# A build-time list scheduler that may place SBUF arithmetic on either of two engines

## The chip, the cores and the metric

The kernel runs on one core of a Trainium2 chip. The metric is the device time of one execution in microseconds. Five engines work side by side, each from its own queue of instructions in a fixed order: TensorE (PE in the profile; PEld are its weight loads), VectorE (DVE), ScalarE (ACT), GpSimd (POOL) and SyncE (SP), which issues all the DMA transfers of this kernel. An instruction waits for semaphores that other engines raise; everything behind it in its queue waits with it.

## The reference

One inference step of a decoder layer, in float32, for a prompt of 2048 tokens and for 8 decode tokens that share the weights. `D_MODEL` is 1024, the FFN width 2816. Cut to what matters:

```python
def decoder_layer(x, ...):
    y = parallel_mixer(rms_norm(x, norm_mix), ...)     # one input projection, then
                                                       #   group A: GLU, depthwise conv of width 31, layer norm, silu
                                                       #   group B: short conv, gated DeltaNet in chunks, 4 heads
                                                       #   concatenated, one output projection
    x = x + y
    x = x + memory_attend(rms_norm(x, norm_mem_q), mem_k, mem_v, w_mq, w_mo)   # 4 heads, 256 memory tokens
    x = x + swiglu(rms_norm(x, norm_ffn), w_gate, w_up, w_down)
    return x, ...

def swiglu(h, w_gate, w_up, w_down):
    return (jax.nn.silu(h @ w_gate) * (h @ w_up)) @ w_down

y_prompt = rms_norm(xp, norm_f)
y_sample = rms_norm(xs, norm_f)
```

## The kernel before

Activations lie transposed, channels on the 128 partitions and tokens along the free axis. The prompt is cut into four blocks of 512 tokens (`NB`, `TB`). Each large product is made of three matmuls in a reduced-precision float32 format: an operand X is split into a high part, which ScalarE writes as a rounded copy, and a low part X - high, which is a subtraction of 128x512 elements from SBUF to SBUF. So each weight tile goes through three steps: a DMA into a `raw` tile, a copy on ScalarE into the first half of a `w` tile, and the subtraction `w<-raw,w` into the second half. Activations are split in the same way (`hT`, `catS`, `op`, `ff`, `fo`), from PSUM or from SBUF.

The FFN uses a seven-product scheme (Strassen's, in Winograd's form) on halves of the tokens and of the channels: products Q1, Q2, P5, P6, Q3, Q7 and P4 per column step `f` (22 steps per block) go to the PSUM tiles `fx`, `fy`, `fz`, and VectorE adds them up into `ffu` and `ffs`. The sums of weights that the scheme needs are `raw<-raw,raw` and `raw<-raw` additions. Those of gate and up are made once and kept in DRAM as `sums`; those of the down projection are made anew in blocks 1 to 3, four operations of 128x128 in a row (`sums_down`). Beside this stand the convolution (`cacc`, 30 taps of 128x512 on VectorE for each of 16 tiles), the DeltaNet chunks with their small triangular inverses (`bit`, `biq`, `Tm`), the norms (sums of squares `sqj`; a power function that only GpSimd runs, for `rs`, `rs1`, `tbr`, `s12`) and the softmax of the memory attention.

No instruction is issued when its line runs. `hybrid_step` drives a rough model of the clock (`Clock`, `Engine`, `Sched`) that decides what is emitted in which order, and each call lands on a `Tape` as an operation with its engine. The engine is set by the code: `V` for VectorE, `G` for GpSimd, or for weight splits and sums a choice between them by the rough clock (`WS.engine`, `WS.split`, `split_down`, `sums_down`). At the end `Tape.issue` calls `Tape.order`, which simulates the five engines, and all instructions go out in the order that it returns; every profile row therefore bears that line, L479.

`order` is a list scheduler. `graph` finds the dependences; `keys` gives each operation a number by which it is needed (for TensorE its place on the tape; for others the smallest number among what depends on it or wants its buffer, at most `LATER` = 300 behind its own). Each engine has a heap `future` of operations by the time at which they will be ready, and a heap `avail` of ready ones by key. The engine whose clock is lowest takes the ready operation with the smallest key whose tiles are to be had; otherwise the operation is put off (`push`) or parked until a buffer of that kind comes free (`wake`). Times come from `Tape.cost`, which returns nanoseconds, whether the operation uses the SBUF port that VectorE and GpSimd share, and a ScalarE table. Operations that use the port follow one another in the plan (`port_at`). Before, every GpSimd operation other than `memset` and `affine_select` counts as a user, and on VectorE those with two tensor inputs in SBUF (`big > 1`). If VectorE's next operation would wait over 150 ns for the port, one that doesn't use it is taken in its place.

What the order fixes: the sequence on each engine, SP's DMA issues among them. What the plan supposes of times has no force on the chip; there only the semaphores decide.

Names in the profile: `w` weight tiles, `raw` their sources, `tbd`/`tbr` and `dnb` the small broadcast of the decode tokens' norm, `nrs` a scaled copy of a norm, `x` the residual, `dn`, `dx`, `dy`, `dz` products of the down projection, `rg` those of the output and attention projections, `sc` scores, `pss` and `prs` sums of squares and their spread on TensorE.

## Time and profile before

| | |
|---|---|
| median of 3 runs | 2961.06 us (2959.1 to 2961.39) |
| the profiled execution's own time | 2956.49 us |
| its span in the profile | 2954.8 us |
| PE, PEld busy | 2901.7 us, 2606.9 us |
| DVE, ACT, POOL busy | 2135.4 us, 1460.3 us, 1832.3 us |
| share of the DMA queue of 16 engines' span | 60.0% |
| mean granted TensorE clock | 0.994 |

A row of the groups of instructions reads: line, engine, operation, written tile <- read tiles, shapes, count | busy time, mean ns of one | idle time of the engine just before them, and what ended it. A row of the waits reads: who <- for whom: us in total, times, the longest. A row of the order of time reads: start, length, engine, operation, count. The span is what the instructions cover; the execution's own time is 1.7 us longer.

### The profile page before, as it was taken

How to read it: one execution, taken by the hardware profiler on the slowest of the kernel's cores; microseconds unless marked ns; L12 is line 12 of the kernel's file. 1: busy time of each engine (PE TensorE's matmuls, PEld its weight loads, DVE VectorE, ACT ScalarE, POOL GpSimd, SP SyncE). 2: the span in 40 equal slices, each digit the busy share in tenths (PEclk: the TensorE clock that was granted, in tenths of full speed). 3: DMA queues.
4: the chain of work that ended last, by engine and by line, in shares of the span. 5: the costliest groups of instructions: out<-in, count | busy, mean ns of one | idle time of the engine just before them, and what ended most of it. 6: DMA issues, size and time to landing. Idle time of an engine off the chain costs nothing.

```text
span 2954.8 us, 56193 instructions
## 1 busy us (share of the span) xinstructions
PE 2901.7 (98%) x19620; PEld 2606.9 (88%) x19620; DVE 2135.4 (72%) x4265; ACT 1460.3 (49%) x3038; POOL 1832.3 (62%) x1949
## 2 busy tenths in 40 slices
PE   9999999999999999999999999999999999999998
PEld 7999878878887888998887888998988999999998
DVE  8757888979758837957577965666866576776667
ACT  7544556456774445455454443444444444444444
POOL 4554454786656455568666127787513888758887
PEclk9999999999999999999999999999999999999999
DMA  6533435777773325766576777777527666666664
GB/s 216 159 95 111 127 107 161 248 250 247 232 237 117 118 86 191 233 193 213 187 248 235 250 242 224 240 232 235 181 91 221 209 202 189 211 227 195 211 210 127
DMA packets 363036, 569.43 MB, mean 193 GB/s; under 512 B 55840, under 2 KB 158560, under 8 KB 362736
## 3 DMA queue, kind: packets, MB, share of 16 engines
q1 hardware_dynamic: 362752, 565.84, 60.0%
q8 instruction: 155, 2.54, 0.3%
q14 instruction: 129, 1.06, 0.1%
HBM read 457.77 MB, written 108.51 MB: 192 GB/s over the span
## 4 chain that ended last, share of the span: by engine, by line
PE 62%; DMA 2%; DVE 1%; POOL 1%; issue 1%; ACT 1%; SPq 0%; POOLq 0%; DVEq 0%; ACTq 0%
PE fy L479 12%; PE rg L479 11%; PE fz L479 8%; PE fx L479 8%; PE dn L479 6%; PE sc L479 5%; PE dx L479 5%; PE dz L479 3%; PE dy L479 1%; DMA w<-sums 1%; PE pu L479 1%; PE pch L479 1%; POOL w L479 0%; PE ppt L479 0%; DMA raw<-in_w_down_dram 0%
## 5 line engine op out<-in xcount | busy, mean ns | idle before, releaser
L479 POOL TENSOR_TENSOR w<-raw,w 128x512 fp32r<-128x512 f32 (+1 forms) x783 | 1040.4, 1339 | 543.7 <-ACT w L479 518.5
L479 ACT ACTIVATE w<-raw 128x512 fp32r<-128x512 f32 (+1 forms) x1066 | 649.5, 619 | 908.4 <-PE fz L479 95.2
L479 PE MATMUL fy<-op,w 128*128 128x256 f32 (+1 forms) x3168 | 435.0, 283 | 6.7 <-DMA w<-sums 3.0
L479 PEld LDWEIGHTS fy<-op,w 128*128 128x128 f32 x3168 | 400.0, 189 | 14.5 <-DVE ffu L479 3.8
L479 PE MATMUL hd<-hT,w 128*128 128x512 f32 (+2 forms) x1920 | 395.9, 356 | 0.6 <-ACT w L479 0.3
L479 DVE SCALAR_TENSOR_TENSOR cacc<-cu,cw,cacc 128x512 f32<-128x512 f32 x480 | 359.2, 748 | 11.6 <-ACT cacc L479 4.9
L479 PEld LDWEIGHTS hd<-hT,w 128*128 128x128 f32 x1920 | 302.3, 188 | 44.1 <-ACT w L479 0.9
L479 DVE TENSOR_TENSOR w<-raw,w 128x512 fp32r<-128x512 f32 (+1 forms) x283 | 251.1, 891 | 90.8 <-ACT w L479 86.8
L479 PE MATMUL fx<-op,w 128*128 128x256 f32 (+1 forms) x2112 | 300.3, 285 | 3.2 <-ACT ffs L479 2.3
L479 PE MATMUL fz<-op,w 128*128 128x256 f32 (+1 forms) x2112 | 292.0, 284 | 1.6 <-DMA w<-sums 1.5
L479 POOL TENSOR_TENSOR sqj<-sqj,sqj 128x512 f32<-128x512 f32 (+1 forms) x98 | 135.0, 1377 | 252.4 <-ACT sqj L479 250.1
L479 PEld LDWEIGHTS fx<-op,w 128*128 128x128 f32 x2112 | 271.5, 190 | 13.7 <-ACT ffs L479 4.3
L479 PEld LDWEIGHTS fz<-op,w 128*128 128x128 f32 x2112 | 268.6, 190 | 8.0 <-issue 4.8
L479 POOL TENSOR_TENSOR raw<-raw 128x128 f32<-128x128 f32 x336 | 194.5, 590 | 21.2 <-DMA raw<-in_w_down_dram 19.9
L479 PE MATMUL dx<-fo,w 128*128 128x256 f32 (+1 forms) x1344 | 197.0, 284 | 0.1
L479 PE MATMUL dn<-ff,w 128*128 128x512 f32 (+2 forms) x960 | 192.5, 352 | 2.8 <-POOL w L479 1.5
L479 PE MATMUL rg<-pT,w 128*128 128x512 f32 x768 | 190.5, 399 | 0.9 <-ACT pr L479 0.7
L479 PE MATMUL sc<-w,hT 128*128 128x512 f32 x768 | 188.6, 401 | 0.0
L479 PE MATMUL rg<-catS,w 128*128 128x512 f32 (+2 forms) x960 | 186.5, 351 | 0.0
L479 POOL TENSOR_TENSOR raw<-raw,raw 128x128 f32<-128x128 f32 (+1 forms) x183 | 161.5, 884 | 28.2 <-PE dr L479 7.1
L479 PEld LDWEIGHTS dx<-fo,w 128*128 128x128 f32 x1344 | 173.8, 188 | 4.0 <-DVE x L479 1.2
L479 PEld LDWEIGHTS rg<-catS,w 128*128 128x128 f32 x960 | 154.4, 188 | 24.6
(401 smaller groups left out, 5060.1 us busy)
## 6 DMA issues: line engine op xcount, KB each, us to landing
w<-sums SPq DMA_DIRECT2D x222, 512.0 KB, 4.3
raw<-in_w_gate_dram SPq DMA_DIRECT2D x192, 256.0 KB, 3.3
sums<-w SPq DMA_DIRECT2D x66, 512.0 KB, 3.8
raw<-in_w_up_dram SPq DMA_DIRECT2D x118, 256.0 KB, 3.6
raw<-in_w_down_dram SPq DMA_DIRECT2D x224, 128.0 KB, 2.7
raw<-in_w_in_dram SPq DMA_DIRECT2D x96, 256.0 KB, 3.2
raw<-sums SPq DMA_DIRECT2D x74, 256.0 KB, 3.3
raw<-wk SPq DMA_DIRECT2D x64, 256.0 KB, 2.8
```

The costliest lines, as they stand in the source:

```text
L479: fn(*args, **kw)
```

## The change

Three things change in the scheduler, and nothing in what is computed.

1. *Either engine.* A `tensor_tensor` addition, subtraction or multiplication on VectorE or GpSimd whose output has at least `FLEX` = 64 elements per partition and that touches no PSUM gets a second form for the other engine, with its cost (`Tape.other`). `order` pushes it into the heaps of both; the first that takes it has it (`gone`, `given`), and `issue` calls that engine's function. The engine that the code named no longer matters for these operations. As consumers they become ready by the later of the two engines' latencies.
2. *The rule for GpSimd.* When GpSimd chooses, `taken` adds up VectorE's load: how far its clock is ahead, and the cost of all ready operations in its heap. Only if this is over `BACKLOG` = 1800 ns may GpSimd take a movable operation. Otherwise the operation is taken off GpSimd's heap, stays with VectorE, and its cost is added to the load for the next one looked at. Operations that only GpSimd can run are taken as before.
3. *Costs.* On VectorE, `tensor_copy` and `tensor_scalar` with neither input nor output in PSUM and more than 2 elements count as users of the shared port. The cost of a GpSimd operation is 150 + 2.15 n ns for a `tensor_tensor` (before 135 + 2.14 n), and 150 + 3.4 n for the others.

```diff
@@ -74,6 +74,8 @@
 NRAW = 11
 
 LATER = 300
+FLEX = 64
+BACKLOG = 1800
 
 
 class Clock:
@@ -164,6 +166,7 @@
 
     def __init__(self):
         self.ops, self.tag_of, self.bufs, self.psum = [], {}, {}, set()
+        self.real, self.other, self.given = {}, {}, {}
 
     def pool(self, pool, bufs, psum=False):
         return TapePool(self, pool, bufs, psum)
@@ -178,6 +181,10 @@
             outs = [kw[k] for k in ("out", "accum_out") if kw.get(k) is not None]
             ins = [v for k, v in kw.items() if k not in ("out", "accum_out") and hasattr(v, "name") and hasattr(v, "shape")]
         self.ops.append((eng, op, fn, args, kw, outs, ins, self.cost(eng, op, args, kw, outs, ins)))
+        two = {"dve": "pool", "pool": "dve"}.get(eng)
+        if two in self.real and op == "tensor_tensor" and kw.get("op") in (ALU.add, ALU.subtract, ALU.mult):
+            if elems(outs[0]) >= FLEX and not any(a.name in self.psum for a in outs + ins):
+                self.other[len(self.ops) - 1] = two, getattr(self.real[two], op), self.cost(two, op, args, kw, outs, ins)
 
     def cost(self, eng, op, args, kw, outs, ins):
 
@@ -205,12 +212,13 @@
         if eng == "dve":
             ptr = any(hasattr(kw.get(k), "shape") for k in ("scalar", "scalar1"))
             half = op in ("tensor_copy", "tensor_scalar") and not psum_in
-            return 68 + (61 if ptr else 0) + n * (6.2 if op == "reciprocal" else 0.525 if half else 1.042), big > 1, None
+            shared = big > 1 or (half and n > 2 and not any(a.name in self.psum for a in outs))
+            return 68 + (61 if ptr else 0) + n * (6.2 if op == "reciprocal" else 0.525 if half else 1.042), shared, None
         if kw.get("op") == ALU.pow:
             return 280 + 180 * n, True, None
         if op in ("memset", "affine_select"):
             return 40 + 0.85 * n, False, None
-        return 135 + n * (2.14 if op == "tensor_tensor" else 3.4), True, None
+        return 150 + n * (2.15 if op == "tensor_tensor" else 3.4), True, None
 
     def box(self, a):
 
@@ -350,13 +358,27 @@
 
         start, end, ends = [0.0] * N, [0.0] * N, {}
 
+        gone = [False] * N
+
         def push(n):
             heappush(future[self.ops[n][0]], (ready[n], key[n], n))
+            if n in self.other:
+                heappush(future[self.other[n][0]], (ready[n], key[n], n))
+
+        def cost(n, e):
+            return self.ops[n][7] if e == self.ops[n][0] else self.other[n][2]
+
+        def taken(t):
+            load = max(0.0, clock["dve"] - t)
+            for _, m in avail["dve"]:
+                if not gone[m]:
+                    load += cost(m, "dve")[0]
+            return load
 
         def wake(tag, t):
-            for n in parked[tag]:
+            for e, n in parked[tag]:
                 ready[n] = max(ready[n], t)
-                push(n)
+                heappush(future[e], (ready[n], key[n], n))
             parked[tag].clear()
 
         for n in range(N):
@@ -381,13 +403,23 @@
                 _, k, n = heappop(fu)
                 heappush(av, (k, n))
             skipped = []
+            load = taken(t) if e == "pool" else 0.0
+            busy = e != "pool" or load > BACKLOG
             n = None
             while av:
                 k, n = heappop(av)
+                if gone[n]:
+                    n = None
+                    continue
+                if not busy and n in self.other:
+                    load += cost(n, "dve")[0]
+                    busy = load > BACKLOG
+                    n = None
+                    continue
                 at_ = bank_at(n, e)
                 if at_ > t:
                     ready[n] = at_
-                    push(n)
+                    heappush(fu, (ready[n], key[n], n))
                     n = None
                     continue
                 new = [x for x in tiles[n] if x not in given]
@@ -399,9 +431,9 @@
                     elif free[tag][0] > t:
                         stop = tag, free[tag][0]
                 if stop is None:
-                    if e == "dve" and self.ops[n][7][1] and port_at > t + 150 and not skipped:
-
-                        other = [(k2, m) for k2, m in av if not self.ops[m][7][1] and all(x in given for x in tiles[m]) and bank_at(m, e) <= t]
+                    if e == "dve" and cost(n, e)[1] and port_at > t + 150 and not skipped:
+
+                        other = [(k2, m) for k2, m in av if not gone[m] and not cost(m, e)[1] and all(x in given for x in tiles[m]) and bank_at(m, e) <= t]
                         if other:
                             skipped.append((k, n))
                             k, n = min(other)
@@ -410,10 +442,10 @@
                             new = []
                     break
                 if stop[1] is None:
-                    parked[stop[0]].append(n)
+                    parked[stop[0]].append((e, n))
                 else:
                     ready[n] = stop[1]
-                    push(n)
+                    heappush(fu, (ready[n], key[n], n))
                 n = None
             for x in skipped:
                 heappush(av, x)
@@ -432,7 +464,9 @@
                     early[tag].add(at[x])
                 if parked[tag]:
                     wake(tag, t)
-            ns, port, tb = self.ops[n][7]
+            ns, port, tb = cost(n, e)
+            gone[n] = True
+            self.given[n] = e
             s = t
             if port and e in ("dve", "pool"):
                 s = max(s, port_at)
@@ -457,7 +491,7 @@
             lat = self.LAT["dma" if e == "sp" else e]
             for m in succs[n]:
                 left[m] -= 1
-                ready[m] = max(ready[m], fin + lat[self.ops[m][0]])
+                ready[m] = max(ready[m], fin + (max(lat["dve"], lat["pool"]) if m in self.other else lat[self.ops[m][0]]))
                 if not left[m]:
                     push(m)
             for x in tiles[n]:
@@ -475,7 +509,9 @@
     def issue(self, tc):
         with tc.manual_schedule():
             for n in self.order():
-                _, _, fn, args, kw, *_ = self.ops[n]
+                eng, _, fn, args, kw, *_ = self.ops[n]
+                if self.given[n] != eng:
+                    fn = self.other[n][1]
                 fn(*args, **kw)
 
 
@@ -603,6 +639,7 @@
     nc = tc.nc
     C = Clock()
     tape = Tape()
+    tape.real = {"dve": nc.vector, "pool": nc.gpsimd}
     GS, PE, SP = tape.port(nc.gpsimd, "pool"), tape.port(nc.tensor, "pe"), tape.port(nc.sync, "sp")
     V, A, G = Engine(tape.port(nc.vector, "dve"), "dve", C), Engine(tape.port(nc.scalar, "act"), "act", C), Engine(GS, "pool", C)
     S = Sched(C)
```

## The prediction

> **What bounds the kernel now.** I began with the page: the head, the busy shares, the granted clock.
>
> ```profile
> span 2954.8 us, 56193 instructions
> PE 2901.7 (98%) x19620; PEld 2606.9 (88%) x19620; DVE 2135.4 (72%) x4265; ACT 1460.3 (49%) x3038; POOL 1832.3 (62%) x1949
> ```
>
> TensorE is busy for all but 53.1 us. An edit that touches only VectorE (DVE) and GpSimd (POOL) can win no more than TensorE's waits and what follows from them, and can lose much more. So the second view is that of TensorE's waits, longest sum first (total, times, longest).
>
> ```profile
> PE dnb L479 <- DVE tbd L479: 7.1, 2, 6.1
> PE pu L479 <- DMA Tm<-zt: 4.7, 3, 3.0
> PE fy L479 <- DMA w<-sums: 3.0, 3, 1.6
> PE pss L479 <- DVE sqj L479: 2.8, 1, 2.8
> PE fx L479 <- ACT ffs L479: 2.3, 2, 1.9
> PE pch L479 <- DVE chr L479: 1.9, 4, 0.9
> PE fy L479 <- DVE ffu L479: 1.8, 2, 1.0
> PE ptw L479 <- DVE Tm L479: 1.6, 1, 1.6
> PE dn L479 <- POOL w L479: 1.5, 1, 1.5
> PE pu L479 <- DVE u L479: 1.5, 1, 1.5
> PE fy L479 <- DVE w L479: 1.2, 1, 1.2
> PE wk L479 <- POOL w L479: 0.8, 1, 0.8
> PE fx L479 <- POOL w L479: 0.3, 1, 0.3
> ```
>
> No wait dominates. Most end on VectorE or GpSimd. The third view is the instructions in order of time, around the longest wait and around a second place of its kind.
>
> ```profile
> 2061.92 6.16 DVE L479 TENSOR_SCALAR tbd<-ident,tbr 8x8 f32<-8x8 f32 x1
> 2061.86 1.26 POOL L479 TENSOR_TENSOR w<-raw,w 128x512 fp32r<-128x512 f32 x1
> 2064.32 2.08 POOL L479 TENSOR_TENSOR raw<-raw 128x128 f32<-128x128 f32 x5
> 2067.61 0.44 POOL L479 TENSOR_TENSOR raw<-raw 128x128 f32<-128x128 f32 x1
> 918.93 3.65 DVE L479 TENSOR_SCALAR nrs<-rs 128x4 f32<-128x4 f32 x1
> 918.49 3.80 POOL L479 TENSOR_TENSOR w<-raw,w 128x512 fp32r<-128x512 f32 x3
> ```
>
> An 8x8 `tensor_scalar` lasted 6.16 us, from just behind the start of a GpSimd subtraction to the end of an unbroken row of GpSimd operations; a 128x4 one lasted 3.65 us beside three subtractions. The planner of before counts neither as a user of the port: it asks for two SBUF tensor inputs, and these have one.
>
> The Trainium skill ("SBUF — State Buffer", Who interferes with whom) says that whoever starts first holds the shared pair for its instruction and the other blocks until that one ends. By that rule the wait would end with the first GpSimd instruction, 1.26 us after its start, and about 5 us of the first term below would not exist. The row shows a wait through many instructions, so the row is used.
>
> Last, the clock and the pace by stage (columns: length, busy time of PE, PEld, DVE, ACT, POOL with counts, granted clock, DMA share, GB/s).
>
> ```profile
> 1350.00:1425.00 75.00, 69.47 (x480) 64.85 (x479) 49.67 (x104) 36.91 (x84) 59.69 (x61) 0.93 0.58 188
> 2025.00:2100.00 75.00, 68.36 (x562) 65.68 (x561) 51.24 (x91) 35.56 (x68) 55.76 (x71) 0.95 0.68 221
> 1740.00:2110.00 370.00, 361.30 (x2882) 338.80 (x2881) 223.88 (x426) 157.74 (x304) 268.45 (x302) 0.99 0.72 231
> 2250.00:2570.00 320.00, 317.21 (x2572) 313.51 (x2571) 208.38 (x465) 140.89 (x276) 257.50 (x274) 0.99 0.69 213
> ```
>
> The slices with the long waits also have the lowest clock: 75 x 0.05 = 3.8 us lost at 2025, 75 x 0.07 = 5.2 at 1350. The two last rows are two FFN passes: 370/2882 = 128.4 ns and 320/2572 = 124.4 ns per matmul.
>
> **The change part by part.** *Movable work.* SBUF sums, differences and products from 64 elements on may go to either engine, and GpSimd takes one only when more than 1.8 us of VectorE work is counted. What it holds now, and what VectorE would take for it:
>
> ```profile
> L479 POOL TENSOR_TENSOR w<-raw,w 128x512 fp32r<-128x512 f32 x698 | 949.1, 1368 | 497.8 <-ACT w L479 473.5 <-DMA w<-sums 4.0 <-DMA raw<-in_w_outq_dram 3.6
> L479 POOL TENSOR_TENSOR raw<-raw 128x128 f32<-128x128 f32 x336 | 194.5, 590 | 21.2 <-DMA raw<-in_w_down_dram 19.9 <-DVE w L479 0.6
> L479 POOL TENSOR_TENSOR sqj<-sqj,sqj 128x512 f32<-128x512 f32 x90 | 129.1, 1434 | 246.3 <-ACT sqj L479 244.3
> L479 POOL TENSOR_TENSOR raw<-raw,raw 128x512 f32<-128x512 f32 x71 | 97.1, 1370 | 26.6 <-PE dr L479 7.1 <-DMA raw<-in_w_up_dram 5.7 <-PE pch L479 4.2
> L479 POOL TENSOR_TENSOR w<-raw,w 128x384 fp32r<-128x384 f32 x85 | 92.8, 1096 | 45.9 <-ACT w L479 45.0 <-DVE ffu L479 0.4
> L479 POOL TENSOR_TENSOR raw<-raw,raw 128x128 f32<-128x128 f32 x112 | 64.5, 576 | 1.6 <-DMA raw<-in_w_down_dram 1.6
> L479 DVE TENSOR_TENSOR sqj<-sqj,sqj 128x512 f32<-128x512 f32 x18 | 12.5, 697 | 3.8 <-POOL sqj L479 2.0 <-ACT sqj L479 1.7
> L479 DVE TENSOR_TENSOR w<-raw,w 128x512 fp32r<-128x512 f32 x256 | 220.1, 864 | 82.4 <-ACT w L479 78.4 <-DMA raw<-in_w_outq_dram 2.2 <-POOL w L479 0.6
> 2061.40 0.41 DVE L479 TENSOR_TENSOR ffs<-ffu,ffu 128x256 f32<-128x256 f32 x1
> ```
>
> The six GpSimd rows hold 1527 us. On VectorE a 128x512 operation takes between 0.697 (the row almost free of port waits) and 0.864 us; a 128x128 one has no row, and I bound it by 0.41 us, the 128x256 row, from above and a quarter of 0.697 = 0.17 from below, and take 0.3. All of it at VectorE: (698 + 90 + 71) x 0.697 = 599, 85 x at most 0.697 = 59, 448 x 0.3 = 134, together 792 us; 2135 + 792 = 2927 of 2955 would leave VectorE no slack, so the 1.8 us rule must send a part back. How much, no row shows: between nothing and all moves. I take half, because VectorE has 819 us of idle time in all: +396 us there, -763 us at GpSimd. Port waits inside VectorE's time fall as well: (864 - 697) x 256 = 43 us on this one row; for all rows I take 80. That gives VectorE 2135 + 396 - 80 = 2451 us (83%) and GpSimd about 1070 (36%). None of that is time by itself; it lies beside TensorE.
>
> *Truer port account.* Fast `tensor_copy` and `tensor_scalar` with over 2 elements now claim the port in the plan; GpSimd's fixed cost rises from 135 to 150 ns. These alter only the order of issue and cost no instruction. No DMA is added or removed, but the loads are ordered by when the plan frees their buffers, so SP's queue is reordered too; DMA waits of TensorE (7.7 us in the two rows quoted) are taken as unchanged, between 0 and twice that.
>
> *New waits.* A movable operation on VectorE stands in one queue with the PSUM evacuations. The queue is sorted by need, so an evacuation waits for at most the operation in progress, 0.7 us, or 0.7 + 1.3 = 2.0 us where that one waits for a GpSimd operation. Twelve matmuls, which make one FFN product for a quarter of the operands, take 12 x 124.4 ns = 1.5 us at the pace of the 2250 row; three banks turn round, so I estimate the room before a bank is wanted again as at least two such pieces, 3.0 us. So the cover holds; without it every microsecond over 3.0 is TensorE's.
>
> *The sum.* In us, with both ends: `tbd` waits -6 (0 to -7.1), since an 8x8 operation no longer stands beside a row of GpSimd work; the clock behind it -3.8 (0 to -3.8). The clock at 1350: the chain there contains GpSimd's own power function, which stays, so -2 (0 to -5.2). Subtractions that TensorE waited for, 1.5 + 0.8 + 0.3: -2 (0 to -2.6). The end, `pss` behind the last sum of squares: -2 (0 to -2.8). Late VectorE results (`ffu`, `Tm`, `chr`, `u`, `w` 1.2, and `ffs`): 10.3 in all, half: -5 (+5 to -10). The pace of the pass at 1740: 2882 x 4.0 ns = 11.5, less the 6.1 and 3.8 already counted, -1 (0 to -1.6). New stalls of a VectorE at 83%: +6 (0 to +33, the price of the second rival). Together -15.8 us.
>
> The profiled execution took 2956.5 us, its span 2954.8; the median of the runs is 2961.06, 4.6 above it. 2956.5 - 15.8 + 4.6 = 2945.3, so about 2945 us, 0.5% faster.
>
> **The rivals.**
> *Stalls move.* TensorE is issued in an order fixed by the plan, and every reordering makes new places where plan and chip differ. The waits are many and, but for one of 6.1, at most 3.0 us long: as many may come as go. Here belongs also that the change does not do what it says: if busy stretches always hold over 1.8 us of ready VectorE work, GpSimd keeps its load and little changes. Against it: VectorE is idle for 28% of the span. Time: 2961, within 0.2% (5.9 us, about what a measurement can tell from no change).
>
> *VectorE becomes the bound of the FFN passes.* At 2250 to 2570 VectorE has 208 us and GpSimd 257 of 320. If four fifths moved, at about half the time each, VectorE would hold 208 + 0.8 x 257 x 0.51 = 313 of 320 us, and with 1.8 us of queue plus a blocked 1.3 us operation an evacuation that is not taken out of turn waits 3.1 us, over the 3.0 of room; from there it decides. With two blocked operations it is 4.4. The excess, 0.1 to 1.4, is 0.75 in the middle; on half of the 88 FFN column steps (22 in four passes) that is 33 us. Of the gains only those on `tbd`, its clock and the subtractions stay, 6 + 3.8 + 2 = 12: 2961 + 33 - 12 = 2982. For it: GpSimd is the busier engine in every FFN row. Against it: queue order by need.
>
> *A larger gain.* If a plan that counts the port rightly also meets the waits on DMA and ScalarE, two thirds of the 53.1 us idle and all 9 us of the two slow slices go: 2956.5 - 35 - 9 + 4.6 = 2917. Against it: it asks that no new wait appears.
> The Trainium skill ("Perfetto Trace Analysis", Identifying the Most-Contended Engine) calls matmul busy time a poor measure of headroom and LDWEIGHTS busy share a good one. By that, the 88% of PEld rather than the 98% of PE is the headroom, which speaks for this rival; that the two passes differ in pace at full PE agrees.
>
> **How the numbers follow.** Forecast (2926 to 2955) 0.54; larger gain 0.08; stalls move 0.15; VectorE bound 0.23. Faster by over 0.2%: 0.54 + 0.08 = 0.62; same 0.15; slower 0.23. The forecast's own range is 2926 to 2955; the range for 8 in 10 reaches to 2918 below, at the edge of the larger gain, and to 2972 above, which leaves out the worse half of the slower case.
>
> **What would show it.** Right: GpSimd near 36% and VectorE near 83%; mean of VectorE's w<-raw,w nearer 0.70 than 0.86; no `tensor_scalar` of several us; the `tbd` wait gone and the 2025 slice at clock 1.00; PE's idle sum near 40 us. Wrong: VectorE at 90% with PE waiting for `ffu`, `ffs` or `x`; PE idle above 55 us; new rows of DMA waits; GpSimd still above 55%.

## The result, and the profile after

| | before | after |
|---|---|---|
| median, runs of both taken side by side | 2959.1 us (2955.42 to 2961.39) | 2938.16 us (2932.24 to 2944.51) |
| the profiled execution | 2956.49 us | 2932.24 us |
| PE idle in it | 53.1 us | 39.6 us |
| mean granted TensorE clock | 0.994 | 0.998 |

The ratio of after to before is 0.9931, with an interval of 0.9911 to 0.995: 0.7% faster, for a forecast of 0.5%. The head of the page of after (all rows that follow bear the line of its `issue`, L515):

```profile
span 2930.5 us, 55769 instructions
PE 2890.9 (99%) x19620; PEld 2598.0 (89%) x19620; DVE 2470.0 (84%) x5364; ACT 1452.0 (50%) x3034; POOL 754.0 (26%) x850
```

The profiled executions differ by 24.3 us. With the same 19,620 matmuls, TensorE's idle time fell by 53.1 - 39.6 = 13.5 us, and its busy time by 2901.7 - 2890.9 = 10.8 us. The mean clock fits the second part: 0.004 x 2954.8 = 11.8 us. So a little over half of the gain is waits, and the rest goes with the clock. In the trace of before the granted clock has two values only, 1.00 and 0.50. It is at 0.50 in five stretches (3.4 us from 930, 10.2 from 1404.6, 3.4 from 1579, 6.8 from 2066.8 and 3.4 from 2493) and in the last 7 us, and each of the five begins inside a wait of TensorE of 1 us or more, or at most 1.1 us behind the end of one. In after one such stretch is left, 3.4 us from 647, beside the last 7 us. The stretch behind the longest wait of before (length, busy time of PE, PEld, DVE, ACT, POOL with counts, clock, DMA share, GB/s):

```profile
2066.80:2073.60 6.80, 4.84 (x22) 4.78 (x23) 3.57 (x8) 1.18 (x3) 1.25 (x4) 0.50 0.07 11
```

TensorE's waits in after, the largest rows and those that answer to rows of before (total, times, longest):

```profile
PE wk L515 <- ACT jn L515: 4.2, 5, 1.2
PE sc L515 <- ACT pr L515: 3.6, 3, 2.0
PE vp L515 <- ACT jn L515: 3.3, 3, 1.4
PE pss L515 <- DVE sqj L515: 2.1, 2, 1.8
PE fz L515 <- DMA w<-sums: 1.7, 3, 1.0
PE pch L515 <- DVE chr L515: 1.3, 3, 0.6
PE ptw L515 <- DVE Tm L515: 1.2, 1, 1.2
PE dnb L515 <- DVE tbd L515: 0.2, 1, 0.2
```

The 7.1 us on `tbd` are 0.2; no wait on a subtraction and none on `Tm<-zt` is left. The new head of the list is ScalarE: `wk` and `vp` (products that are made once for the memory attention) waiting for `jn`, the tile that ScalarE copies them to, and `sc` for `pr`, the softmax's exponentials, 11.1 us, of which before had 1.4:

```profile
PE wk L479 <- ACT jn L479: 0.8, 1, 0.8
PE vp L479 <- ACT jn L479: 0.6, 1, 0.6
```

All of TensorE's waits on transfers were 9.2 us in before (`Tm<-zt` 4.7, `w<-sums` 3.0 and 1.5) and are 1.7 in after.

What moved, in groups kept apart by shape:

```profile
L515 DVE TENSOR_TENSOR w<-raw,w 128x512 fp32r<-128x512 f32 x762 | 554.6, 732 | 150.3 <-ACT w L515 146.9 <-DMA w<-sums 0.5 <-DMA xpark<-x 0.2
L515 POOL TENSOR_TENSOR w<-raw,w 128x512 fp32r<-128x512 f32 x192 | 267.5, 1398 | 326.3 <-ACT w L515 272.7 <-issue 20.3 <-DVE catS L515 10.1
L515 DVE TENSOR_TENSOR raw<-raw 128x128 f32<-128x128 f32 x306 | 86.1, 292 | 13.9 <-DMA raw<-in_w_down_dram 10.1 <-issue 1.9 <-POOL w L515 0.9
```

Of the 698 large weight subtractions GpSimd kept 192: 72% moved, and of the 336 sums of 128x128 even 91%. A subtraction lasts 0.732 us on VectorE (0.864 before) where it lasts 1.398 on GpSimd, and a small sum 0.292 where it lasted 0.590.

The place of the longest wait, in order of time:

```profile
2056.09 0.54 POOL L515 TENSOR_TENSOR tbr<-tbm,ex 8x1 f32<-8x1 f32 x1 [64.56 <-DVE tbm L515]
2056.68 0.21 DVE L515 TENSOR_SCALAR tbd<-ident,tbr 8x8 f32<-8x8 f32 x1
2057.14 0.88 DVE L515 TENSOR_TENSOR raw<-raw 128x128 f32<-128x128 f32 x4
```

`tbd` takes 0.21 us instead of 6.16. GpSimd had been idle for 64.56 us ahead of `tbr` and has nothing to put behind it; the small sums stand on VectorE, behind `tbd`.

The n-th matmul of a tile name is the same piece of work in every kernel, so it can serve as a mark of time. Between such marks lie the first three of the four FFN passes, each from just behind its start to its end (bounds rounded to a microsecond; columns as above). The passes of before:

```profile
1181.00:1587.00 406.00, 395.17 (x2854) 362.17 (x2853) 293.25 (x538) 206.20 (x465) 274.44 (x247) 0.98 0.67 220
1759.00:2096.00 337.00, 328.30 (x2654) 309.16 (x2654) 205.17 (x388) 144.07 (x281) 253.23 (x287) 0.99 0.72 232
2267.00:2570.00 303.00, 300.21 (x2462) 298.05 (x2462) 201.30 (x454) 134.72 (x266) 250.91 (x269) 0.99 0.68 211
```

The same passes of after, and the two slices that had the lowest clock:

```profile
1183.00:1576.00 393.00, 388.90 (x2845) 355.86 (x2844) 338.40 (x665) 205.26 (x463) 103.33 (x116) 1.00 0.70 229
1753.00:2080.00 327.00, 325.29 (x2647) 306.29 (x2646) 264.75 (x661) 142.10 (x280) 13.79 (x17) 1.00 0.73 237
2252.00:2549.00 297.00, 296.87 (x2464) 296.20 (x2464) 252.33 (x644) 134.23 (x265) 89.19 (x81) 1.00 0.69 215
1350.00:1425.00 75.00, 73.47 (x532) 68.25 (x531) 65.59 (x145) 40.35 (x91) 29.93 (x36) 1.00 0.64 209
2025.00:2100.00 75.00, 73.86 (x591) 70.19 (x591) 65.72 (x145) 38.74 (x75) 30.25 (x26) 1.00 0.73 233
```

All of the gain lies here: 406 to 393, 337 to 327, 303 to 297, by the exact marks 27.6 us. In the second pass TensorE's idle time goes from 8.7 to 1.7 us and its busy time from 328.3 to 325.3. GpSimd falls from 253 to 14 us, and VectorE has only 265 of 327. The other stages give 3.3 us back: the mixer, up to 1183, takes 1.5 us more and the stages behind the three passes 3.7, 1.0 and 0.4 more, while the tail, which holds the fourth pass, takes 3.3 less.

In the stage between the first two passes a new clash can be seen. The 32 products `kt<-kt,qb` of the decode tokens' attention were all on VectorE before; now GpSimd takes 22 of them.

```profile
1667.76 7.97 POOL L515 TENSOR_TENSOR kt<-kt,qb 128x512 f32<-128x512 f32 x6
1674.49 0.56 ACT L515 ACTIVATE pr<-sc,mx,rs 128x256 f32<-128x256 f32 x1 [2.41 <-POOL kt L515]
1675.74 0.50 PE L515 MATMUL sc<-w,hT 128*128 128x512 f32 x1 [1.97 <-ACT pr L515]
```

The products are slower there, ScalarE is put down as waiting for them, and TensorE waits for ScalarE: the 2.0 us of the row `sc <- pr`.

### The profile page after: what moved, and what is told of

It reads as the page before. It is cut to its first block, busy times and chain, and to the rows that moved or that the text cites. A ratio compares the mean times of both kernels' runs of the same rounds, so it can differ in the third digit from the quotient of the medians.

```text
span 2930.5 us, 55769 instructions
## 1 busy us (share of the span) xinstructions
PE 2890.9 (99%) x19620; PEld 2598.0 (89%) x19620; DVE 2470.0 (84%) x5364; ACT 1452.0 (50%) x3034; POOL 754.0 (26%) x850
## 4 chain that ended last, share of the span: by engine, by line
PE 51%; DVE 2%; DMA 2%; ACT 1%; issue 1%; POOL 0%; SPq 0%; POOLq 0%; DVEq 0%; ACTq 0%
PE fy L515 11%; PE fz L515 8%; PE fx L515 7%; PE rg L515 6%; PE dx L515 5%; PE dn L515 5%; PE dz L515 3%; PE sc L515 3%; PE dy L515 1%; DMA w<-sums 1%; DVE w L515 1%; PE pu L515 0%; PE podd L515 0%; DVE x L515 0%; PE pch L515 0%
## 5 line engine op out<-in xcount | busy, mean ns | idle before, releaser
L515 ACT ACTIVATE w<-raw 128x512 fp32r<-128x512 f32 (+1 forms) x1066 | 649.5, 619 | 888.9 <-issue 138.2
L515 DVE TENSOR_TENSOR w<-raw,w 128x512 fp32r<-128x512 f32 (+1 forms) x861 | 610.8, 713 | 161.5 <-ACT w L515 156.8
L515 PE MATMUL fy<-op,w 128*128 128x256 f32 (+1 forms) x3168 | 434.3, 282 | 0.1
L515 PEld LDWEIGHTS fy<-op,w 128*128 128x128 f32 x3168 | 399.1, 188 | 7.6 <-issue 1.8
L515 PE MATMUL hd<-hT,w 128*128 128x512 f32 (+2 forms) x1920 | 394.2, 356 | 1.0 <-DVE hT L515 0.5
L515 POOL TENSOR_TENSOR w<-raw,w 128x512 fp32r<-128x512 f32 (+1 forms) x205 | 282.5, 1382 | 341.7 <-ACT w L515 277.9
L515 DVE SCALAR_TENSOR_TENSOR cacc<-cu,cw,cacc 128x512 f32<-128x512 f32 x480 | 357.6, 745 | 9.2 <-ACT cacc L515 5.7
L515 PEld LDWEIGHTS hd<-hT,w 128*128 128x128 f32 x1920 | 302.6, 188 | 45.4 <-ACT w L515 1.2
L515 PE MATMUL fx<-op,w 128*128 128x256 f32 (+1 forms) x2112 | 297.3, 283 | 0.3
L515 PE MATMUL fz<-op,w 128*128 128x256 f32 (+1 forms) x2112 | 285.8, 283 | 1.8 <-DMA w<-sums 1.7
L515 PEld LDWEIGHTS fx<-op,w 128*128 128x128 f32 x2112 | 269.4, 189 | 8.3 <-ACT w L515 3.4
L515 PEld LDWEIGHTS fz<-op,w 128*128 128x128 f32 x2112 | 264.5, 188 | 9.0 <-issue 4.8
L515 PE MATMUL dx<-fo,w 128*128 128x256 f32 (+1 forms) x1344 | 197.8, 283 | 0.7 <-DVE x L515 0.6
L515 PE MATMUL rg<-pT,w 128*128 128x512 f32 x768 | 191.3, 400 | 2.1 <-ACT pr L515 0.9
L515 PE MATMUL dn<-ff,w 128*128 128x512 f32 (+2 forms) x960 | 192.0, 353 | 0.3 <-ACT ffs L515 0.2
L515 PE MATMUL sc<-w,hT 128*128 128x512 f32 x768 | 188.5, 399 | 3.6 <-ACT pr L515 3.6
L515 PE MATMUL rg<-catS,w 128*128 128x512 f32 (+2 forms) x960 | 186.2, 351 | 0.0
L515 PEld LDWEIGHTS dx<-fo,w 128*128 128x128 f32 x1344 | 174.7, 188 | 2.7 <-DVE x L515 1.3
L515 PEld LDWEIGHTS rg<-catS,w 128*128 128x128 f32 x960 | 154.6, 188 | 24.6
L515 PEld LDWEIGHTS sc<-w,hT 128*128 128x128 f32 x768 | 141.4, 188 | 36.8 <-ACT pr L515 5.9
L515 PEld LDWEIGHTS rg<-pT,w 128*128 128x128 f32 x768 | 140.5, 188 | 35.8 <-ACT pr L515 2.2
L515 PEld LDWEIGHTS dn<-ff,w 128*128 128x128 f32 x960 | 150.9, 188 | 22.0 <-DVE ffs L515 0.5
```

The lines of the kernel that those rows point to most:

```text
L515: fn(*args, **kw)
```

## The experiments

All ratios are to before, run beside each kernel (medians 2958.7 to 2960.7). "FFN" is the time from matmul number 10 to number 2400 of `fy` (counted from 0), which spans the first three passes, what lies between them and the way to the fourth; "mixer" is the time from the span's start to matmul number 10. Both are of the profiled execution.

| kernel | median us | ratio (interval) | mixer | FFN |
|---|---|---|---|---|
| before | 2959.1 | | 1181.3 | 1435.3 |
| after | 2938.16 | 0.9931 (0.9911 to 0.995) | 1182.8 | 1412.8 |
| `costs_only` | 2954.26 | 0.9979 (0.9968 to 0.999) | 1173.3 | 1433.8 |
| `moves_only` | 2930.06 | 0.9902 (0.9886 to 0.9917) | 1180.4 | 1408.8 |
| `no_backlog_limit` | 2942.19 | 0.9943 (0.993 to 0.9955) | 1180.6 | 1422.8 |
| `backlog_zero` | 2950.66 | 0.997 (0.996 to 0.998) | 1179.7 | 1429.2 |
| `tbd_on_act` | 2974.45 | 1.0051 (1.0037 to 1.0065) | 1184.3 | 1454.5 |
| `same_plan_sums_dve` | 2973.81 | 1.0048 (1.0034 to 1.0062) | 1184.5 | 1442.7 |
| `same_plan_all_dve` | 3049.54 | 1.0306 (1.029 to 1.0322) | 1249.8 | 1452.7 |
| `plan_shift_before` | 2959.53 | 0.9998 (0.9988 to 1.0009) | 1192.2 | 1425.0 |
| `plan_shift_after` | 2935.41 | 0.9923 (0.991 to 0.9936) | 1188.7 | 1410.4 |
| `moves_and_port_flag` | 2936.89 | 0.9927 (0.9913 to 0.9941) | 1186.9 | 1414.0 |
| `moves_limit_1700` | 2946.13 | 0.9956 (0.9943 to 0.9969) | 1192.6 | 1418.4 |
| `two_limits` | 2941.56 | 0.9939 (0.9925 to 0.9953) | 1194.4 | 1409.4 |

### Each half of the change alone

`costs_only` is after with nothing movable; `moves_only` is after with the costs and the port account of before.

```diff
 # costs_only
-        if two in self.real and op == "tensor_tensor" and ...
+        if False and two in self.real and op == "tensor_tensor" and ...
 # moves_only
-            shared = big > 1 or (half and n > 2 and not any(a.name in self.psum for a in outs))
+            shared = big > 1
-        return 150 + n * (2.15 if op == "tensor_tensor" else 3.4), True, None
+        return 135 + n * (2.14 if op == "tensor_tensor" else 3.4), True, None
```

> Only the third part of the change: the new costs and the fuller account of the shared port, every operation on the engine that the code names. Theory A (the gain comes from work that leaves GpSimd): no gain beyond the scatter of a new order, 2950 to 2966 us, GpSimd busy near 1830 us, VectorE near 2130. Rival B (the gain comes from a plan that knows the port better): 2945 us or less. Rival C (any new order of issue is worth several us either way): outside both, below 2950 or above 2966, with other places of waiting.

> The first two parts without the third: either engine, rule of 1.8 us, costs and port account as before. A: 2930 to 2947 us, VectorE near 2470, GpSimd near 750 us busy, the 6 us wait for tbd gone. B: 2950 us or more. C: 2930 to 2960, but the slow places elsewhere than in the changed kernel.

The head of the page of `costs_only`:

```profile
PE 2901.5 (98%) x19620; PEld 2607.5 (88%) x19620; DVE 2120.0 (72%) x4265; ACT 1463.3 (50%) x3042; POOL 1821.9 (62%) x1949
```

The same of `moves_only`:

```profile
PE 2891.8 (99%) x19620; PEld 2600.0 (89%) x19620; DVE 2478.6 (85%) x5373; ACT 1454.4 (50%) x3037; POOL 758.0 (26%) x841
```

Both lie in the ranges of theory A, `moves_only` at its very edge and in that of C as well. The truer account alone leaves the engines as they were and brings 0.2%, 6 us (8.0 in the mixer and 1.5 in the FFN, of which the tail gives some 3 back). The moves alone bring 29 us, more than the whole change, and are the fastest kernel that was run. So most of the gain is the moves'. That the account takes something away from them is not shown: further down, 100 ns of the limit move a kernel by more than the 8 us between `moves_only` and after.

One place doesn't belong to the moves alone. In `costs_only` the `tbd` of the second pass is short too, with all sums still on GpSimd:

```profile
2059.38 0.22 DVE L515 TENSOR_SCALAR tbd<-ident,tbr 8x8 f32<-8x8 f32 x1
```

By the marks that place gives 8.0 us there, as much as in after. Other losses, in the first pass and in the tail, hide it in the total. Whether the account or the mere new order took the row away from `tbd` is open; the new order of `plan_shift_before`, below, did not.

### The limit of 1.8 us

Without it VectorE gets every movable operation; at -1 GpSimd takes each operation that it can, first come first served.

```diff
 # no_backlog_limit
-BACKLOG = 1800
+BACKLOG = 1e12
 # backlog_zero
-BACKLOG = 1800
+BACKLOG = -1
```

> The changed kernel with a limit that is never reached: VectorE takes every movable operation. If VectorE can become the bound: busy about 2750 us (93%), TensorE waits for ffu, ffs, x or sums, 2950 to 3000 us. If the rule's share for GpSimd is not needed: 2925 to 2942 us with VectorE near 2650 us, GpSimd under 250 us.

> The changed kernel with a limit below zero: GpSimd takes any movable operation as soon as it is free, the two engines share the work first come, first served. A: GpSimd back to 1400 to 1800 us busy, VectorE's mean for w<-raw,w again over 0.8 us, most of the gain lost, 2948 to 2965 us. B (the account of the port is what matters): 2932 to 2945 us.

One slice near the start of the first pass, in `no_backlog_limit` (columns as in the windows above):

```profile
1200.00:1275.00 75.00, 67.80 (x442) 59.55 (x440) 74.98 (x157) 30.76 (x67) 7.50 (x14) 0.95 0.55 169
```

And in after:

```profile
1200.00:1275.00 75.00, 74.04 (x532) 68.39 (x532) 69.29 (x149) 36.73 (x74) 43.21 (x47) 1.00 0.69 205
```

Without the limit VectorE is busy for 74.98 of 75 us; TensorE issues 442 matmuls instead of 532, at a clock of 0.95. By the marks some 15 us are lost against after between 1245 and 1270 us. It is the stretch in which the convolution's taps stand in VectorE's queue beside the FFN's evacuations. That is the second rival's mechanism at one place, though here VectorE is simply full and hardly blocked (GpSimd 7.5 us). With the limit GpSimd does 43 us of work in the same slice, and the loss is not there. Over the whole kernel VectorE is far from full:

```profile
PE 2897.2 (98%) x19620; PEld 2601.2 (88%) x19620; DVE 2546.0 (87%) x5821; ACT 1445.4 (49%) x3029; POOL 188.8 (6%) x393
```

Both expectations had it busier (2750 and 2650 us), and the time falls between their ranges. The median is 4 us above that of after, which is less than two orders can differ by, as the last group of runs shows. So the limit is shown to matter at this place, and not for the total.

The other end, `backlog_zero`, head and groups by shape:

```profile
PE 2899.1 (98%) x19620; PEld 2601.1 (88%) x19620; DVE 2337.9 (79%) x4464; ACT 1454.1 (49%) x3035; POOL 1738.5 (59%) x1750
L515 POOL TENSOR_TENSOR w<-raw,w 128x512 fp32r<-128x512 f32 x526 | 726.4, 1385 | 636.6 <-ACT w L515 570.1 <-DVE pr L515 15.6 <-DVE x L515 12.7
L515 DVE TENSOR_TENSOR w<-raw,w 128x512 fp32r<-128x512 f32 x428 | 402.0, 941 | 161.3 <-ACT w L515 155.4 <-DMA wk<-jn 2.2 <-issue 0.6
```

A free choice of engine, without the rule, brings 0.3%. GpSimd keeps 1738 us, and VectorE's subtraction is at 0.941 us, dearer than before. The expectation of theory A held in all its parts. All seven orders in which VectorE is the default, with a limit or without, are faster (2930 to 2946 us). That speaks for the default; but the free choice was run in one order only, 4.5 us from the nearest of them. That letting GpSimd take the overflow pays beside the default is not shown.

### Is it the row of GpSimd work that blocks, or the small operation?

Three kernels start from before and change only who does what. `tbd_on_act` makes `tbd` on ScalarE, which also makes a new order. `same_plan_sums_dve` sends the 448 sums of 128x128 to VectorE when they are issued, at the places that the plan had given them on GpSimd; `same_plan_all_dve` does that with all movable operations from 64 elements on. The last two leave the order untouched. (Only the lines that decide are shown.)

```diff
 # tbd_on_act
-        V.tensor_scalar(out=dg[:n, :n], in0=ident[:n, :n], scalar1=r[:n, :], scalar2=None, op0=ALU.mult)
+        A.activation(out=dg[:n, :n], in_=ident[:n, :n], func=AF.Copy, scale=r[:n, :])
 # same_plan_sums_dve, in Tape.issue
+                if eng == "pool" and op == "tensor_tensor" and kw.get("op") in (ALU.add, ALU.subtract, ALU.mult) and elems(outs[0]) == 128 and all(a.name.startswith("raw") for a in outs + ins):
+                    fn = self.vector.tensor_tensor
 # same_plan_all_dve, in Tape.issue
+                if eng == "pool" and op == "tensor_tensor" and kw.get("op") in (ALU.add, ALU.subtract, ALU.mult) and elems(outs[0]) >= 64:
+                    fn = self.vector.tensor_tensor
```

> The kernel before with one edit: the scaled identity tbd, the 8x8 operation that took 6.16 us on VectorE, is made on ScalarE, which doesn't use the shared port. If the blocked operation is the cause of its term: the 6.1 us wait of dnb and the low clock behind it go, 6 to 10 us at that place, 2950 to 2955 us in all. If the wait only hands on to another late operation: under 3 us at that place, 2957 to 2963 us.

> The order of before, unchanged; only the 448 sums and differences of 128x128 that build the down projection's weights are issued to VectorE instead of GpSimd, at the same place of the order. Theory: the long block at 2062 us came from an unbroken row of these on GpSimd. Then the 6 us wait there goes (tbd under 2 us) and 6 to 10 us are won between 2060 and 2090; over the passes from 1740 on VectorE gains about 126 us of work without a plan for it, which costs some us: 2948 to 2962 us in all. If a row of GpSimd work is not the cause: the wait for tbd stays at several us, 2958 us or more.

> The plan of before, order of issue unchanged, but each GpSimd sum, difference or product of 64 or more elements is issued to VectorE at the same place of the order. No part of the plan knows of it. If faster operations and a free port suffice: 2930 to 2950 us. If the move pays only where the order is made for it (VectorE's queue now has long work in front of evacuations): 2965 us or more, with TensorE waiting for ffu, x and raw.

The place of `tbd` in `tbd_on_act`, in order of time:

```profile
2081.07 6.51 DVE L479 TENSOR_TENSOR ffs<-ffu,ffs 128x256 f32<-128x256 f32 x1
2081.09 1.26 POOL L479 TENSOR_TENSOR w<-raw,w 128x512 fp32r<-128x512 f32 x1
2081.15 0.30 ACT L479 ACTIVATE tbd<-ident,tbr 8x8 f32<-8x8 f32 x1 [0.32 <-POOL tbr L479]
...
2083.55 2.09 POOL L479 TENSOR_TENSOR raw<-raw 128x128 f32<-128x128 f32 x5
...
2086.85 0.45 POOL L479 TENSOR_TENSOR raw<-raw 128x128 f32<-128x128 f32 x1
```

`tbd` is out of the way in 0.30 us, and the block falls on VectorE's next operation, `ffs<-ffu,ffs`, with 6.51 us to the end of the same row of GpSimd work. A row of its waits shows the price:

```profile
PE fx L479 <- ACT ffu L479: 8.1, 2, 6.6
```

So of the two expectations the second is right at this place: the wait was handed on, and the stretch from 3 us ahead of the operation to 14 us behind it has the same busy time and the same clock of 0.80 as in before. Both totals were missed, by 11 us and more; the 23 us that the profiled execution lost lie at other places of the new order, 20 of them by the marks ahead of 1700 us. Two things follow. The wait belongs to the row of GpSimd operations and not to `tbd`. Nor are only operations hit that the plan does not count: `ffs<-ffu,ffs` has two SBUF inputs and is a user of the port in this plan too.

The same place in `same_plan_sums_dve`, where the row behind the subtraction is gone:

```profile
2067.73 1.27 POOL L481 TENSOR_TENSOR w<-raw,w 128x512 fp32r<-128x512 f32 x1
2067.79 1.24 DVE L481 TENSOR_SCALAR tbd<-ident,tbr 8x8 f32<-8x8 f32 x1
```

`tbd` waits for the one operation in progress, 1.24 us, and by the marks 5.4 us are won around it. That settles the cause of the long block. The total was missed all the same, by 12 us: behind 2251 us, where the kernel stood level with before by the marks, 18.1 us are lost up to the end. That stretch in before and in this kernel, and its largest new wait:

```profile
2262.00:2954.00 692.00, 677.04 (x5618) 671.33 (x5616) 468.09 (x1017) 302.10 (x592) 546.36 (x592) 0.99 0.64 201
2262.00:2973.00 711.00, 689.96 (x5618) 675.27 (x5616) 529.45 (x1305) 302.72 (x592) 384.42 (x304) 0.99 0.63 196
PE dx L481 <- DVE xd L481: 3.2, 6, 0.8
```

About 6 us of it are idle time of TensorE. The other 13 are busy time of the same 5618 matmuls at the same mean clock, which no run explains. That VectorE's queue had not been planned to hold these sums is the likely reason, but it is argued and not shown. `same_plan_all_dve` loses much more. Its head and its first waits:

```profile
PE 2938.6 (96%) x19620; PEld 2615.8 (86%) x19620; DVE 2561.1 (84%) x5821; ACT 1460.9 (48%) x3038; POOL 190.6 (6%) x393
PE pu L481 <- DVE u L481: 10.8, 2, 9.7
PE pch L481 <- DVE S L481: 7.1, 6, 3.6
```

VectorE is as busy as in after, 84%, and GpSimd, which shares the port, at only 6%, and the kernel is 3.1% slower, as its second expectation had it. The waits are on `u`, `S` and sums of squares, though, and not on the `ffu`, `x` and `raw` that were expected, and three quarters of the loss, 69 us, lie in the mixer. So in this kernel the faster engine brought nothing where the order was not made anew with it.

### How much is the luck of an order?

Five kernels change numbers of the plan. `plan_shift_before` is before with one nanosecond on the cost of GpSimd; `plan_shift_after` and `moves_limit_1700` lower the limit to 1700 in after and in `moves_only`; `moves_and_port_flag` is after with the old cost line of GpSimd; `two_limits` is `moves_only` with a limit of -1 in the first 720 us of the plan, to see whether the mixer wants GpSimd's help.

```diff
 # plan_shift_before
-        return 135 + n * (2.14 if op == "tensor_tensor" else 3.4), True, None
+        return 136 + n * (2.14 if op == "tensor_tensor" else 3.4), True, None
 # plan_shift_after, moves_limit_1700
-BACKLOG = 1800
+BACKLOG = 1700
 # moves_and_port_flag
-        return 150 + n * (2.15 if op == "tensor_tensor" else 3.4), True, None
+        return 135 + n * (2.14 if op == "tensor_tensor" else 3.4), True, None
 # two_limits, beside the old costs (BACKLOG inside the loop becomes limit too)
-            busy = e != "pool" or load > BACKLOG
+            limit = -1 if t < 720e3 else BACKLOG
+            busy = e != "pool" or load > limit
```

> The kernel before with one constant of its plan changed by a nanosecond (a GpSimd operation counted as 136 instead of 135 ns): a new order of issue that has no reason to be better. It measures what a new order is worth by itself. Theory A: within 5 us of before. Rival C (luck of the order): as far away as the changed kernel, 20 us, either way.

> The changed kernel with a limit of 1700 instead of 1800 ns. A: 2930 to 2945 us, a spread of some us around the changed kernel. C: 2945 us or more, the limit was a lucky one.

> Either engine with the costs of before, limit 1700 instead of 1800 ns. If the old costs are better together with the moves: 2926 to 2934 us again. If the 8 us between that kernel and the changed one are luck of the order: 2934 to 2944 us.

> The changed kernel with GpSimd's old cost (135 + 2.14 n): only the fuller account of the port is left of its third part. If the account of the port is what loses the 8 us: 2936 to 2942 us. If GpSimd's new cost loses them: 2927 to 2934 us. If neither: between or outside, by luck of the order.

> Either engine with the costs of before; for the first 720 us of the plan GpSimd takes whatever it can (limit below zero), then 1800 ns as in the change. If the mixer's first part, where VectorE is the busier engine and every kernel with the 1.8 us rule lost 1 to 7 us against before, wants GpSimd's help: the mark at the end of the mixer's products at -1 us or better against before in place of +7, and 2920 to 2928 us in all. If those us are luck of the order: 2928 to 2940 us.

One nanosecond left the total of before as it was and still changed its inside. TensorE's waits in `plan_shift_before`:

```profile
PE pu L479 <- DVE u L479: 9.4, 2, 8.1
PE dnb L479 <- DVE tbd L479: 7.1, 2, 6.2
```

A wait of 8.1 us that before does not have came up in the mixer, where the marks fall behind by 14.9 us at 695 us, and 10 us were won back in the FFN; the wait on `tbd` is there again. 100 ns of the limit are worth -2.8 us to after and +16.1 to `moves_only`, which misses both ranges of `moves_limit_1700`. In `two_limits` the mixer became 13 us longer and not shorter: that idea fell, and both of its ranges were missed. `moves_and_port_flag` landed in the range that blames the account of the port, but beside a scatter of that size this proves nothing. So a difference of some 8 us (0.3%) between two orders of this kind, or even of 16, says nothing of their rules.

The gain itself stands out of that scatter, though not by much. The six kernels with the moves and a limit near 1.8 us have medians of 2930 to 2946, 2938 in the mean. The three that keep the engines of before with a plan of their own (before, `costs_only`, `plan_shift_before`) have 2954 to 2960, 2958 in the mean. No member of one group reaches into the other. In the FFN they take 1409 to 1418 us against 1425 to 1435, 19 us apart in the mean; in the mixer the groups overlap. By the marks of each pass they overlap in the first as well (391 to 397 us, but 390 in `plan_shift_before`). Apart are the second (326 to 329 against 330 to 338, the 330 being `costs_only`) and, most clearly, the third (296 to 298 against 303 to 304).

## Why the prediction was right, and which terms were not

The time came out, 2938.16 us in the forecast's own range and 7 us below the 2945, and so did the main lines of the mechanism: work leaves GpSimd, the rows and the waits behind them go, and the clock comes back. Some terms met their number by luck, and one gain was not in the sum. The terms, in the order of the sum:

- *The `tbd` waits, the clock behind them and the pace of that pass*, -10.8 in three terms: right. The pass took 9 us less, the wait went from 7.1 to 0.2 us, and the slice at 2025 from a clock of 0.95 to 1.00. The reason given, a row of GpSimd work and not the operation, was shown by `tbd_on_act` and `same_plan_sums_dve`. But the moves are not needed for it: `costs_only`, without them, won the same 8.0 us at this place.
- *The clock at 1350*, -2: mis-sized. The whole of it went (0.93 to 1.00, the far end of that term), and the wait on `Tm<-zt` of 3.0 us at this place, which the prediction had left among the unchanged DMA waits, went with it. By the marks the place gave about 9 us. GpSimd's power function stayed, but the subtractions in the queue around it did not. More widely, the prediction priced the clock in two slices, at 5.8 us, and missed the three stretches of 3.4 us elsewhere; over the span TensorE's busy time fell by 10.8.
- *DMA waits, taken as unchanged*, 0: missed. Both rows that were quoted, 7.7 us, are gone, and of all waits on transfers 1.7 of 9.2 us are left. That is more than the `tbd` waits gave, and it can't be credited to the moves: one nanosecond of the plan, in `plan_shift_before`, brought the 9.2 to 4.7.
- *Subtractions*, -2, at most -2.6: none of those three waits is left.
- *The end*, -2: -1.3 from the start of the last `dn` matmul to the end of the span, of which `pss` gives 1.0 (2.8 to 1.8; the other 0.3 of its row in after lie near the first pass).
- *Late VectorE results*, -5: the size was right. The same names (`Tm`, `chr`, `u` and what else was listed) hold some 5 us after 10.3. One was misread: by its row, the 2.3 us of `ffs` end on ScalarE. 1.9 of them stood in the third pass, which took 6.7 us less; the sum had no term for that pass. Of the rest there, 1.7 us are a stretch of 3.4 us at half the clock that began behind this wait.
- *New stalls*, +6: the size was near, the place was wrong. They came, but not as evacuations late on VectorE. They came as 9.7 us more of TensorE waiting for `jn` and `pr` on ScalarE, ahead of the first pass (`jn`) and between the first two (`pr`). That they come from the moves is not shown; `costs_only`, without moves, waits 4.4 us for `jn`.
- *How much moves*: half was a choice, and it was wrong. Three quarters of the weight subtractions moved (578 of 783 with both shapes), GpSimd is at 754 us and not 1070. That VectorE's 2470 us come close to the 2451 is luck, an agreement of a sum with several wrong terms. Counted by forms, some 1220 operations went to VectorE and 121 from VectorE to GpSimd (`kt`, `hT` and `catS` among them), a direction that the sum doesn't have. The reading behind it, that all movable work would fill VectorE to 2927 us, fell with `no_backlog_limit`: VectorE has all of it there and is busy for 2546 us. The 80 us taken for port waits inside VectorE's time were far too few for that kernel. The prices of single operations were good: a 128x128 sum lasts 0.29 us, as taken, and the subtraction 0.732, nearer to the free 0.697 than to 0.864.

Idle time went down by 13.5 us where the idle terms of the sum make 9, and the clock by 10.8 where they make 5.8 and 1 of pace: both parts were under-sized, the clock by more. The median of after stands 5.9 us above its profiled execution instead of 4.6, since that was the fastest one.

The rivals: *stalls move* is excluded by the interval, though its mechanism is real: it is the scatter between orders, 8 us and once 16. *VectorE becomes the bound* is true of one slice of 75 us and only without the limit. *A larger gain* asked for 35 us of idle time; 13.5 came. The Trainium skill ("Perfetto Trace Analysis", Identifying the Most-Contended Engine) spoke for it; the fastest order that was run is at 2930 us with PEld at 89% and PE at 99%, and no run shows whether more is to be had.

The rule that was weighed, the Trainium skill's ("SBUF — State Buffer", Who interferes with whom: the other blocks until the first instruction ends), is right for most waits and wrong for the dear ones. Counted from the trace of before, 448 VectorE instructions were longer by over 100 ns than the shortest tenth of their form; some 430 of them ended with the GpSimd operation in progress, as the rule says, and the others, 16 to 21 by how closely the ends are read, lasted past at least one more. The worst is `tbd`: 12 GpSimd operations ended while it waited. In after there are 231, of which 7 to 9 lasted longer, two of them (at 1241 and 1389, 3.2 us each) past two further operations. By the rule alone, `tbd` would have been worth some 1 us.

Open is what the truer account is worth together with the moves: with it 2935 to 2938 us in three orders, without it 2930 to 2946 in three. Open too is why some VectorE instructions are passed over and most are not.

## What to carry to other kernels

When two engines share a port, look for unbroken rows of one engine's operations beside a short operation of the other that a third engine waits for: here the price was the length of the row, and moving the victim only handed it to the next instruction. Move work to the faster engine, and make the order anew with the move; the same work moved in the old order cost 3.1%. Before a gain of some tenths of a per cent is credited to a rule of a scheduler, shift one of its numbers by next to nothing and see how far the time moves by itself.

## What the hardware showed that was not expected

A VectorE instruction that waits for the shared port can be passed over by a whole row of GpSimd instructions: 6.16 us for an 8x8 `tensor_scalar`, 6.51 us for a 128x256 addition, where the first GpSimd operation took 1.26 us in both cases; with that operation alone beside it, the same `tbd` took 1.24 us. And the clock was worth nearly as much as the waits: with 13.5 us less of TensorE's idle time, the busy time of the same 19,620 matmuls fell by 10.8 us, and the three FFN passes, at 0.98 and 0.99 before, ran at 1.00. That the one follows from the other was not tested by itself. What speaks for it is that the stretches at 0.50 in before begin in waits or just behind them, and that over the 14 profiled executions the time at 0.50 rises, if not in strict order, with TensorE's idle time: 10 us beside 40 idle in after, 35 beside 53 in before, 45 beside 62 in `tbd_on_act`, 62 beside 108 in `same_plan_all_dve`.
